# One decoder step on one core: one-pass spreading of the samples' B and C, and a round's eight score products issued as one run

## The chip, the cores and the metric

The kernel runs on one core of one Trainium2 chip. Its engines are TensorE (PE in the rows, with its weight loads as PEld), VectorE (DVE), ScalarE (ACT), GpSimd (POOL) and SyncE (SP), whose queue issues most loads. The metric is the device time of one execution in microseconds; lower is better. Three timed runs of the kernel before gave 1047.99, 1053.06 and 1053.59 us, so the median is 1053.06 us. The profiled execution is a fourth one, of 1040.78 us.

## What is computed

One inference step of a two-layer hybrid decoder, for a prompt of 256 tokens and 8 samples of one token each, which share the weights. The part that matters here is one layer's mixer:

```
h = RMSNorm(x) * (1 + sc1) + sh1
proj = h @ w_in                       # q, six K/V sets, gates, z, x/B/C, dt
o_cmp  = attention over compressed blocks
o_slc  = attention over the selected 64-token blocks
o_win  = attention over the last 512 tokens plus self
o_att  = gates[0] * o_cmp + gates[1] * o_slc + gates[2] * o_win
h_new  = h_old * exp(dt * A) + dt * x (outer) B     # per sample and head
y      = h_new . C + d_skip * x ; y = RMSNorm(y * SiLU(z))
x = x + g1 * (concat(o_att, y) @ w_out)
x = x + g2 * ConvFFN(RMSNorm(x) * (1 + sc2) + sh2)
```

For the samples K and V come from pages of 128 tokens (selected branch, 8 pages a sample) and from a window buffer of 512 tokens a sample. The window buffer is also an output, so each sample's 512 KB are loaded and stored.

## The kernel before

**Stages.** A layer runs in this order: modulation and norm, the input projection, the mixer, the output projection, the FFN. In the profiled execution the first layer's mixer lies from about 165 to 300 us and the second one's from about 670 to 800 us. In the mixer five generators are interleaved by a table of letters (`SEQ`, then `CYCLE`): S is `samples` (attention of the 8 samples), P is `prompt` (attention of the prompt, four heads by two branches), M is the state space chain (`space_prompt`, `space_samples`, `gate`), B the prompt's compressed branch, Z the z projection. A scheduler places each engine's instructions in a fixed order at build time; on the chip each engine takes them in that order and waits where an operand is not there.

**S: three rounds.** A round `i` treats 512 keys of each of the 8 samples: rounds 0 and 1 are four pages each of the selected branch, round 2 is the window. `fetch` loads one sample's keys and values of a round into one of 8 slots (`PAGES`, tile `page`); a slot comes free when the round before has used its values, so the loads of round 2 (`in_wst_dram`, 512 KB each) are issued when `values(1, ...)` is done. With each of these loads `fetch` also issues a store of the same tile (`out_wst_dram`, on POOL's queue), which waits for the load. `scores` makes eight products, one for each sample: `qz` of the sample (128 x 32, as weights) with the sample's 128 x 512 keys, in float32. Their results go to four groups of 32 partitions of one PSUM bank (tile `psat`); samples 2c and 2c+1 add up in group c. Then DVE adds the bank to `sc`, the softmax follows, `transposed` turns the weights around (`psmm<-cst,whi`) and `values` multiplies them with the pages (`psmm<-page,wlo`). A float32 product shows as two MATMUL records in the trace.

**M: the samples' state.** `space_samples` turns the samples' B and C (channels 4 and 5 of `xc`) to 8 rows (`bc`), spreads them on a diagonal (`bds`, tile `mam`, 8 rows x 1024) and makes four products of a matrix of ones with `bds`, one for each of B and C and each half of the heads. These bring every sample's B and C to all 128 partitions, 128 x 512 in PSUM each. DVE multiplies them with `dtx` and with the state, POOL updates the state. `gate` then normalises y (products `psat<-s,cst`, then `row`, `rs`) and multiplies it with the second half of `w_out`.

**`together`** (used for the modulation products already) emits a list of products and holds all but the first to the program's order at high priority, so that they stand in a row on PE.

Of the kernel before, what the change touches and what calls it, by code (L numbers as in the profile page):

```python
# [9 lines left out]
F32 = mybir.dt.float32  # L10
F32R = mybir.dt.float32r
I32 = mybir.dt.int32
AF = mybir.ActivationFunctionType
OP = mybir.AluOpType
# [6 lines left out]
NS = 8  # L21
# [16 lines left out]
def _const_array():  # L38

    parts = []  # L40

    def add(name, a):
        a = np.asarray(a, np.float32)
        b = np.zeros((128, a.shape[1]), np.float32)
        b[:a.shape[0]] = a
        CONST_W[name] = (sum(x.shape[1] for x in parts), b.shape[1])
        parts.append(b)

    i = np.arange(128)
    slopes = 2.0 ** -(np.arange(8) + 1.0)  # L50
    r = i
    c4, rr = r // 32, r % 32
    live = rr < 16
    sp, h = rr // 8, rr % 8
    g = h // 4
    smp = 2 * c4 + sp
    slope = np.where(live, slopes[h], 0.0)
    add("ident", np.eye(128))
    add("one", np.ones((128, 1)))
    tri = (i[:, None] <= i[None, :])  # L60
    add("tri", tri)
    add("tneg", np.where(tri, 0.0, -1e30))
    same = (smp[:, None] == smp[None, :]) & (g[:, None] == g[None, :]) & live[:, None] & live[None, :]
    add("two", np.eye(2).reshape(1, 4).repeat(128, 0))
    add("same", same)
    q, k = i[:, None], i[None, :]
    diag = np.where(q >= k, q - k, 1e30)
    add("dist", np.concatenate([diag, 128.0 + q - k, diag], 1))
    n = np.arange(NCMP)
    add("cbias", -slope[:, None] * (PAST - (16 * n + 31))[None])  # L70
    n = np.arange(15)
    pb = np.zeros((128, 8, 2, 15))
    pm = np.zeros((128, 2, 15))
    for qt in range(2):
        dd = (qt * 128 + i)[:, None] - (16 * n + 31)[None]
        pm[:, qt] = dd >= 0
        for hh in range(8):
            pb[:, hh, qt] = np.where(dd >= 0, -slopes[hh] * dd, -1e30)
    add("pbias", pb.reshape(128, 240))
    add("pmask", pm.reshape(128, 30))  # L80
    add("slope", slope[:, None])
    hm = np.zeros((128, 3, 8))
    hm[i, :, h] = live[:, None]
    add("hmask", hm.reshape(128, 24))
    gcol = np.arange(128) // 64
    gm = (g[:, None] == gcol[None]) & live[:, None]
    add("gmask", gm)
    add("rmask", np.stack([live & (sp == s) for s in range(2)], 1))
    sel = np.zeros((8, 128))
    sel[smp[live], i[live]] = 1.0  # L90
    add("sels", sel)
    ov_n, ov_j = np.arange(NCMP), np.arange(16)
    add("overlap", (16 * ov_n[:, None] < 64 * ov_j[None] + 64) & (16 * ov_n[:, None] + 32 > 64 * ov_j[None]))
    add("sum4", np.tile(np.eye(32), (4, 1)))
    add("iota", np.broadcast_to(np.arange(16.0), (128, 16)))
    return np.concatenate(parts, 1)

# [5 lines left out]
def decode_step(ctx, tc, I, O):  # L103
# [20 lines left out]
    V, S, G, PE = [Pinned(*z) for z in (("DVE", nc.vector), ("ACT", nc.scalar), ("POOL", nc.gpsimd), ("PE", nc.tensor))]  # L124
# [40 lines left out]
    def ph(shape, tag, bufs=1, dt=F32):  # L165
        return sb(shape, tag, bufs, dt, pools[-1])
# [9 lines left out]
    K = {n: cst[:, o:o + w] for n, (o, w) in CONST_W.items()}  # L176
    ident, ones = K["ident"], K["one"].to_broadcast([128, 128])
# [12 lines left out]
    qz = sb([NS, 32], "qz")  # L190
    G.memset(qz, 0.0)

    def split(src, hi, lo):

        S.activation(hi, src, AF.Copy)
        V.tensor_tensor(lo, src, hi.bitcast(F32), op=OP.subtract)
# [16 lines left out]
    def together(calls):  # L213

        for n, (out, w, a, start, stop) in enumerate(calls):
            if n == 0:
                PE.matmul(out, w, a, start=start, stop=stop)
                continue
            with tc.high_priority():
                tc.keep_in_program_order(PE.matmul(out, w, a, start=start, stop=stop))  # L220
# [257 lines left out]
    def layer(l, A, pa, early, done, side, fill):  # L478
        p = PAR[l]
# [20 lines left out]
        order = (0, 2, 4, 6, 1, 3, 5, 7)  # L500
        ring = []
# [133 lines left out]
        def samples():  # L635
# [72 lines left out]

            def scores(i, sc):
                o = sx()  # L710
                for n, s in enumerate(order):
                    c = s // 2
                    PE.matmul(o[32 * c:32 * c + 32, :], qz[:, s, :], ring[NS * i + n][0], start=s % 2 == 0, stop=s % 2 == 1)
                V.tensor_tensor(sc, sc, o, op=OP.add)

            def transposed(sc, pT):
# [266 lines left out]
        def mb():  # L983
            return ps("at", BANKS[0])
# [92 lines left out]
        def space_samples():  # L1077
# [19 lines left out]
            S.activation(dec_s, ov_[:, :, 1, :], AF.Copy)  # L1097
            V.tensor_tensor(dtx, dtx, xc[:, 0:4, 259::4], op=OP.mult)
            o = mb()
            for i in range(2):  # L1100
                PE.transpose(o[:8, i * 128:(i + 1) * 128], xc[:, 4 + i, 259::4], ident)
            bc = small([2, 128], 1, "bc")
            S.activation(bc[:8], o[:8, :256].rearrange("p (b n) -> p b n", b=2), AF.Copy)
            ys = small([4, NS], 1, "ys")
            bds = [ph([1024], "mam", 2) for _ in range(2)]
            for g in range(2):
                V.tensor_tensor(bds[g][:8].rearrange("p (b s n) -> p b s n", b=2, s=NS),
                                bc[:8, :, 64 * g:64 * g + 64].unsqueeze(2).to_broadcast([8, 2, NS, 64]),
                                ident[:8, :8].unsqueeze(1).unsqueeze(3).to_broadcast([8, 2, NS, 64]), op=OP.mult)
            for g in range(2):  # L1110
                yield
                h0 = slot("st", [2, NS, 64])
                load(h0, I["ssm"][l, :, 2 * g:2 * g + 2])
                G.tensor_tensor(h0, h0, dec_s[:, 2 * g:2 * g + 2, :].unsqueeze(3).to_broadcast([128, 2, NS, 64]), op=OP.mult)
                u = slot("st", [2, NS, 64])
                for b in range(2):
                    o = mb()
                    PE.matmul(o, ones[:8, :], bds[g][:8, 512 * b:512 * b + 512], start=True, stop=True)
                    yield
                    ov_ = o.rearrange("p (s n) -> p s n", s=NS)  # L1120
                    for i in range(2):
                        if b == 0:
                            V.tensor_tensor(u[:, i], dtx[:, 2 * g + i, :].unsqueeze(2).to_broadcast([128, NS, 64]), ov_,
                                            op=OP.mult)
                        else:
                            V.tensor_tensor(u[:, i], h0[:, i], ov_, op=OP.mult)
                    if b == 0:
                        G.tensor_tensor(h0, h0, u, op=OP.add)
                        store(O["ssms"][l, :, 2 * g:2 * g + 2], h0)
                V.tensor_reduce(ys[:, 2 * g:2 * g + 2, :], u, axis=AX.X, op=OP.add)  # L1130
# [304 lines left out]
```

## Time and profile before

| | |
|---|---|
| timed runs | 1047.99, 1053.06, 1053.59 us (median 1053.06) |
| profiled execution | 1040.78 us, its span 1039.0 us (1.78 us lie around the span) |
| busy share of the span | PE 91%, PEld 77%, DVE 63%, ACT 47%, POOL 16% |
| mean granted TensorE clock | 0.945 of 2.4 GHz |
| DMA | 220.35 MB, mean 212 GB/s |

An engine's busy time says only how long it had an instruction in work. Of PE it also counts instructions that run at the lower clock (0.50, that is 1.2 GHz). What a change is worth is read in the stretch where it acts: which engine the others wait for there, and what ends that engine's own waits.

### The profile page before, as it was taken

How to read it: one execution, taken by the hardware profiler on the slowest of the kernel's cores; microseconds unless marked ns; L12 is line 12 of the kernel's file. 1: busy time of each engine (PE TensorE's matmuls, PEld its weight loads, DVE VectorE, ACT ScalarE, POOL GpSimd, SP SyncE). 2: the span in 40 equal slices, each digit the busy share in tenths (PEclk: the TensorE clock that was granted, in tenths of full speed). 3: DMA queues.
4: the chain of work that ended last, by engine and by line, in shares of the span. 5: the costliest groups of instructions: out<-in, count | busy, mean ns of one | idle time of the engine just before them, and what ended most of it. 6: DMA issues, size and time to landing. Idle time of an engine off the chain costs nothing.

```text
span 1039.0 us, 21345 instructions
## 1 busy us (share of the span) xinstructions
PE 949.7 (91%) x7864; PEld 803.7 (77%) x7864; DVE 650.7 (63%) x1429; ACT 487.4 (47%) x1042; POOL 167.8 (16%) x337
## 2 busy tenths in 40 slices
PE   4599998988997998999999989998999799999996
PEld 2368997653585998999999868875447599999995
DVE  1386643867677665676754575485665687777553
ACT  1356543533444555555634344454244366666441
POOL 2000100225221101001101112031421221111110
PEclk9699999999997999999999989997599899999998
DMA  9987488246757786756675578725283835666651
GB/s 357 313 278 266 158 265 292 94 129 225 270 171 254 232 301 216 238 194 220 210 251 174 183 279 301 244 83 158 91 354 96 330 124 182 183 183 183 194 163 42
DMA packets 101258, 220.35 MB, mean 212 GB/s; under 512 B 11682, under 2 KB 54562, under 8 KB 101026
## 3 DMA queue, kind: packets, MB, share of 16 engines
q1 hardware_dynamic: 97058, 205.28, 59.8%
q0 software_dynamic: 3520, 13.17, 3.1%
q8 instruction: 62, 1.02, 0.4%
q10 hardware_dynamic: 576, 0.54, 0.2%
q14 instruction: 42, 0.34, 0.1%
HBM read 204.70 MB, written 14.25 MB: 211 GB/s over the span
## 4 chain that ended last, share of the span: by engine, by line
PE 76%; DMA 11%; DVE 7%; ACT 3%; issue 2%; SPq 1%; POOL 0%; DVEq 0%; ACTq 0%; POOLq 0%
PE psmm L117 40%; PE psat L117 22%; PE pso L117 10%; PE psfl L117 4%; DMA st<-in_cw_dram 3%; DMA ada<-in_ada_dram 3%; DVE wlo L117 2%; DMA cpg<-in_ada_dram 2%; DMA st<-in_wup_dram 1%; DMA page<-in_wst_dram 1%; DVE s L117 1%; SPq L117 1%; ACT whi L117 1%; DVE rs L117 1%; ACT psc L117 1%
## 5 line engine op out<-in xcount | busy, mean ns | idle before, releaser
L117 DVE TENSOR_TENSOR wlo<-st,whi 128x1024 fp32r<-128x1024 f32 (+1 forms) x204 | 232.7, 1142 | 152.6 <-ACT whi L117 149.1
L117 ACT ACTIVATE whi<-st 128x1024 fp32r<-128x1024 f32 (+1 forms) x204 | 201.6, 990 | 217.5 <-PE psmm L117 150.2
L117 PE MATMUL psmm<-hhi,whi 128*128 128x264 f32 x800 | 233.7, 293 | 3.3 <-ACT whi L117 1.4
L117 PE MATMUL psmm<-hhi,wlo 128*128 128x264 f32 x800 | 228.5, 286 | 1.1 <-DVE wlo L117 1.1
L117 PE MATMUL psmm<-hlo,whi 128*128 128x264 f32 x800 | 228.2, 286 | 0.0
L117 PEld LDWEIGHTS psmm<-hhi,whi 128*128 128x128 f32 x800 | 151.4, 189 | 17.0 <-ACT whi L117 5.2
L117 PEld LDWEIGHTS psmm<-hhi,wlo 128*128 128x128 f32 x800 | 150.9, 189 | 5.2 <-DVE wlo L117 2.4
L117 PEld LDWEIGHTS psmm<-hlo,whi 128*128 128x128 f32 x800 | 151.5, 190 | 2.4 <-issue 2.0
L117 PE MATMUL psmm<-act,whi 128*128 128x264 f32 x704 | 128.5, 284 | 0.0
L117 PEld LDWEIGHTS psmm<-act,whi 128*128 128x128 f32 x704 | 108.9, 188 | 1.6 <-issue 1.6
L117 PE MATMUL psat<-hhi,whi 128*128 128x264 f32 x352 | 100.8, 286 | 2.2 <-ACT whi L117 2.2
L117 PE MATMUL psat<-hhi,wlo 128*128 128x264 f32 x352 | 100.5, 286 | 1.0 <-DVE wlo L117 1.0
L117 PE MATMUL psat<-hlo,whi 128*128 128x264 f32 x352 | 100.6, 286 | 0.0
L117 PE MATMUL psmm<-act,wlo 128*128 128x264 f32 x352 | 99.9, 284 | 0.0
L117 PE MATMUL pso<-whi,cwh 128*128 128x252 f32 x256 | 74.8, 292 | 8.7 <-ACT whi L117 8.0
L117 PE MATMUL pso<-wlo,cwh 128*128 128x252 f32 x256 | 74.1, 290 | 1.8 <-DVE wlo L117 1.8
L117 PE MATMUL pso<-whi,cwl 128*128 128x252 f32 x256 | 73.6, 287 | 0.0
L117 PEld LDWEIGHTS psat<-hhi,whi 128*128 128x128 f32 x352 | 67.1, 191 | 2.5 <-ACT whi L117 2.5
L117 POOL COPY fout<-xr 128x26 f32<-128x26 f32 x44 | 28.1, 639 | 247.0 <-ACT xr L117 247.0
L117 PEld LDWEIGHTS psat<-hhi,wlo 128*128 128x128 f32 x352 | 66.7, 190 | 1.2 <-DVE wlo L117 1.2
L117 PEld LDWEIGHTS psat<-hlo,whi 128*128 128x128 f32 x352 | 67.2, 191 | 0.0
L117 PEld LDWEIGHTS psmm<-act,wlo 128*128 128x128 f32 x352 | 66.1, 188 | 0.0
(305 smaller groups left out, 1579.5 us busy)
## 6 DMA issues: line engine op xcount, KB each, us to landing
st<-in_wup_dram SPq DMA_DIRECT2D x88, 512.0 KB, 3.9
ada<-in_ada_dram SPq DMA_DIRECT2D x80, 512.0 KB, 5.2
st<-in_wdn_dram SPq DMA_DIRECT2D x44, 512.0 KB, 3.6
st<-in_win_dram SPq DMA_DIRECT2D x40, 512.0 KB, 4.9
page<-in_slcc_dram SPq DMA_DIRECT2D x128, 128.0 KB, 2.7
cpg<-in_ada_dram SPq DMA_DIRECT2D x16, 512.0 KB, 9.4
st<-in_cw_dram SPq DMA_DIRECT2D x16, 512.0 KB, 5.9
cpg<-in_cmpc_dram SPq DMA_DIRECT2D x64, 128.0 KB, 3.7
```

The costliest lines, as they stand in the source:

```text
L117: ins = f(*a, **k)
```

## The change

It has two parts and touches nothing else.

1. **B and C in one pass.** The 16 columns of B and C (8 samples each) are split to a high and a low float32r part and laid side by side (`xs`, 16 columns for B and 16 for C). The transposes then give 16 rows, `eye8` (a new 16 x 8 constant) spreads the high and the low row of each sample, `bds` is of float32r with 16 rows, and the matrix of ones is a float32r copy of 16 rows (`oner`). The four products have 16 rows and float32r operands in place of 8 rows and float32.
2. **A round's scores in one run.** The eight products go through `together`, from the last sample's page to the first's; the products of odd samples now start a partition group and those of even samples end it.

```
+    add("eye8", np.tile(np.eye(8), (2, 1)))
...
             def scores(i, sc):
                 o = sx()
-                for n, s in enumerate(order):
-                    c = s // 2
-                    PE.matmul(o[32 * c:32 * c + 32, :], qz[:, s, :], ring[NS * i + n][0], start=s % 2 == 0, stop=s % 2 == 1)
+                together([(o[32 * (s // 2):32 * (s // 2) + 32, :], qz[:, s, :], ring[NS * i + n][0], s % 2 == 1, s % 2 == 0)
+                          for n, s in reversed(list(enumerate(order)))])
                 V.tensor_tensor(sc, sc, o, op=OP.add)
...
             o = mb()
+
+            xs = ph([2, 16], "xs", 1, F32R)
+            split(xc[:, 4:6, 259::4], xs[:, :, :8], xs[:, :, 8:])
             for i in range(2):
-                PE.transpose(o[:8, i * 128:(i + 1) * 128], xc[:, 4 + i, 259::4], ident)
+                PE.transpose(o[:16, i * 128:(i + 1) * 128], xs[:, i, :].bitcast(F32), ident)
             bc = small([2, 128], 1, "bc")
-            S.activation(bc[:8], o[:8, :256].rearrange("p (b n) -> p b n", b=2), AF.Copy)
+            S.activation(bc[:16], o[:16, :256].rearrange("p (b n) -> p b n", b=2), AF.Copy)
+            oner = ph([128], "oner", 1, F32R)
+            S.activation(oner[:16], ones[:16], AF.Copy)
             ys = small([4, NS], 1, "ys")
-            bds = [ph([1024], "mam", 2) for _ in range(2)]
+            bds = [ph([1024], "mam", 2, F32R) for _ in range(2)]
             for g in range(2):
-                V.tensor_tensor(bds[g][:8].rearrange("p (b s n) -> p b s n", b=2, s=NS),
-                                bc[:8, :, 64 * g:64 * g + 64].unsqueeze(2).to_broadcast([8, 2, NS, 64]),
-                                ident[:8, :8].unsqueeze(1).unsqueeze(3).to_broadcast([8, 2, NS, 64]), op=OP.mult)
+                V.tensor_tensor(bds[g][:16].rearrange("p (b s n) -> p b s n", b=2, s=NS),
+                                bc[:16, :, 64 * g:64 * g + 64].unsqueeze(2).to_broadcast([16, 2, NS, 64]),
+                                K["eye8"][:16].unsqueeze(1).unsqueeze(3).to_broadcast([16, 2, NS, 64]), op=OP.mult)
...
-                    PE.matmul(o, ones[:8, :], bds[g][:8, 512 * b:512 * b + 512], start=True, stop=True)
+                    PE.matmul(o, oner[:16, :], bds[g][:16, 512 * b:512 * b + 512], start=True, stop=True)
```

**Where the instructions stand.** In the fences below, `page_n` are the loaded pages; those of one round bear rising numbers in the order of their loads. The first place is PE in the first layer, at round 1. Before:

```order
L117 MATMUL psat_2734<-mam_2692,cst_61 128x512
L117 MATMUL psat_2886<-page_2753,qz_72 32x512
L117 MATMUL psat_2886<-page_2767,qz_72 32x512
L117 MATMUL psat_2886<-page_2781,qz_72 32x512
L117 MATMUL psat_2886<-page_2795,qz_72 32x512
L117 MATMUL pso_2927<-pT_437_2900,vt_1881 64x256
L117 MATMUL psat_2912<-mam_2692,cst_61 128x512
L117 MATMUL psat_2886<-page_2825,qz_72 32x512
L117 MATMUL pso_2927<-pT_439_2906,vt_1881 64x256
L117 MATMUL pso_2927<-pT_437_2900,vt_1881 64x128
L117 MATMUL pso_2927<-pT_439_2906,vt_1881 64x128
L117 MATMUL psat_2942<-mam_2693,cst_61 128x512
```

Four products stand together and the other four singly, among the products of B and C, up to the last one three rows of the prompt's scores later. The same place now:

```order
L118 MATMUL pso_2932<-pT_441_2911,vt_1881 64x128
L118 MATMUL psat_2891<-page_2872,qz_72 32x512
L118 MATMUL psat_2891<-page_2858,qz_72 32x512
L118 MATMUL psat_2891<-page_2844,qz_72 32x512
L118 MATMUL psat_2891<-page_2830,qz_72 32x512
L118 MATMUL psat_2891<-page_2800,qz_72 32x512
L118 MATMUL psat_2891<-page_2786,qz_72 32x512
L118 MATMUL psat_2891<-page_2772,qz_72 32x512
L118 MATMUL psat_2891<-page_2758,qz_72 32x512
L118 MATMUL psat_2917<-mam_2697,oner_2694 128x512
L118 MATMUL psat_2947<-mam_2698,oner_2694 128x512
```

All eight stand in a row, the page that was loaded last (2872) first. Three of the four products of B and C are behind them; the first of these four and the prompt's values stand ahead.

The second place is PE in the first layer at round 2, the window (`pso<-pT` ends the prompt's values, `psat<-s` and `row` are `gate`'s, `pp`, `kv,q` and `vcp` the prompt's). Before:

```order
L117 MATMUL pso_2927<-pT_465_3055,vt_1881 64x128
L117 MATMUL psat_3035<-page_2967,qz_72 32x512
L117 MATMUL psat_3061<-s_467_3065,cst_61 2x264
L117 MATMUL psat_3061<-s_468_3071,cst_61 2x264
L117 MATMUL psat_3035<-page_2970,qz_72 32x512
L117 MATMUL psat_3061<-s_469_3077,cst_61 2x264
L117 MATMUL psat_3061<-s_470_3083,cst_61 2x264
L117 MATMUL psat_3035<-page_2973,qz_72 32x512
L117 MATMUL psat_3087<-cst_61,row_74 128x2 x3
L117 MATMUL psat_3129<-cst_61,pp_2618 15x128 x4
L117 MATMUL psat_3142<-kv_1450,q_1449 128x128
L117 MATMUL psat_3143<-kv_1450,q_1449 128x128
```

The products of the eight pages are spread over some forty rows of other work, one at a time. Now:

```order
L118 MATMUL pso_2932<-pT_467_3060,vt_1881 64x128
L118 MATMUL psat_3040<-page_3009,qz_72 32x512
L118 MATMUL psat_3040<-page_3006,qz_72 32x512
L118 MATMUL psat_3040<-page_3003,qz_72 32x512
L118 MATMUL psat_3040<-page_3000,qz_72 32x512
L118 MATMUL psat_3040<-page_2981,qz_72 32x512
L118 MATMUL psat_3040<-page_2978,qz_72 32x512
L118 MATMUL psat_3040<-page_2975,qz_72 32x512
L118 MATMUL psat_3040<-page_2972,qz_72 32x512
L118 MATMUL psat_3066<-s_469_3070,cst_61 2x264
L118 MATMUL psat_3066<-s_470_3076,cst_61 2x264
L118 MATMUL psat_3066<-s_471_3082,cst_61 2x264
```

The run of eight stands where the first window product stood before, its first row uses the page that is loaded last (3009), and everything that stood between the eight is now behind them. The second layer has the same order here. The loads of the pages keep their place on SP's queue.

The third place is POOL in the first layer, at the stores of the window pages (`psc<-psc,psm` scales the prompt's weights). Before:

```order
L1129 DMA out_ssms_dram<-st_2938 128x1024
L117 TENSOR_SCALAR psc_3009<-psc_3009,psm_3010 128x128
L117 TENSOR_SCALAR psc_3009<-psc_3009,psm_3010 128x256
L117 TENSOR_SCALAR psc_3009<-psc_3009,psm_3010 128x128
L117 TENSOR_SCALAR psc_3009<-psc_3009,psm_3010 128x256
L511 DMA out_wst_dram<-page_2967 128x1024
L511 DMA out_wst_dram<-page_2970 128x1024
```

Now:

```order
L1134 DMA out_ssms_dram<-st_2943 128x1024
L512 DMA out_wst_dram<-page_2972 128x1024
L512 DMA out_wst_dram<-page_2975 128x1024
L118 TENSOR_SCALAR psc_3014<-psc_3014,psm_3015 128x128
L512 DMA out_wst_dram<-page_2978 128x1024
```

In the first layer the stores begin ahead of the prompt's scaling; in the second they did so before already.

## Rows read from the trace of the kernel before

**Rows 1.** The page's chain that ended last, by engine.

```profile
PE 76%; DMA 11%; DVE 7%; ACT 3%; issue 2%; SPq 1%; POOL 0%; DVEq 0%; ACTq 0%; POOLq 0%
```

**Rows 2.** Stretches: length; busy PE, PEld, DVE, ACT, POOL (count); clock; DMA; GB/s.

```profile
254.00:276.00 22.00, 21.42 (x108) 9.96 (x110) 12.34 (x40) 8.36 (x24) 9.24 (x16) 1.00 1.02 396
752.00:774.00 22.00, 19.73 (x88) 8.04 (x89) 13.52 (x42) 7.97 (x22) 6.45 (x12) 1.00 1.02 408
...
728.00:754.00 26.00, 24.91 (x131) 11.26 (x130) 16.75 (x36) 5.93 (x19) 10.48 (x10) 0.56 0.27 96
...
772.00:798.00 26.00, 23.51 (x209) 16.90 (x209) 15.49 (x52) 12.73 (x39) 3.90 (x9) 0.93 0.28 104
```

**Rows 3.** Timeline of PE, first layer, round 1: start, us, instructions, [idle <-releaser].

```profile
230.59 2.04 PE L117 MATMUL psat<-mam,cst 8*128 8x512 f32 x2 [1.73 <-DVE mam L117]
232.56 1.94 PE L117 MATMUL psat<-page,qz 128*32 128x512 f32 x8
...
235.47 1.12 PE L117 MATMUL psat<-mam,cst 8*128 8x512 f32 x2
236.53 1.04 PE L117 MATMUL psat<-page,qz 128*32 128x512 f32 x2
...
243.19 1.05 PE L117 MATMUL psat<-page,qz 128*32 128x512 f32 x2
```

**Rows 4.** Timeline of PE, second layer, rounds 0 and 1.

```profile
692.07 1.06 PE L117 MATMUL psat<-page,qz 128*32 128x512 f32 x8
...
732.29 3.64 PE L117 MATMUL psat<-page,qz 128*32 128x512 f32 x16
735.86 2.07 PE L117 MATMUL psat<-mam,cst 8*128 8x512 f32 x2
```

**Rows 5.** Timeline of PE, first layer, round 2.

```profile
255.94 1.05 PE L117 MATMUL psat<-page,qz 128*32 128x512 f32 x2
...
272.97 1.04 PE L117 MATMUL psat<-page,qz 128*32 128x512 f32 x2
```

**Rows 6.** Timeline of PE, second layer, round 2.

```profile
754.44 1.02 PE L117 MATMUL psat<-page,qz 128*32 128x512 f32 x2 [0.37 <-DVE wlo L117]
756.27 1.04 PE L117 MATMUL psat<-page,qz 128*32 128x512 f32 x2 [0.82 <-DMA page<-in_wst_dram]
...
771.08 1.04 PE L117 MATMUL psat<-page,qz 128*32 128x512 f32 x2
```

**Rows 7.** Last window loads: duration, first and last start; time to landing; first, second layer.

```profile
L117 SPq DMA_DIRECT2D page<-in_wst_dram x1: 412/412/412, 254.7 to 254.7; - x1
...
DMA to landing us min/median/max: 13.0/13.0/13.0
...
L117 SPq DMA_DIRECT2D page<-in_wst_dram x2: 382/470/557, 753.0 to 753.5; - x2
...
DMA to landing us min/median/max: 14.1/15.1/16.1
```

**Rows 8.** The last load of round 1, first layer, in the same view.

```profile
L117 SPq DMA_DIRECT2D page<-in_slcc_dram x1: 332/332/332, 236.3 to 236.3; - x1
...
DMA to landing us min/median/max: 2.6/2.6/2.6
```

**Rows 9.** Timeline of PE: float32r products in a row.

```profile
276.91 0.29 PE L117 MATMUL psmm<-hhi,whi 128*128 128x264 f32 x1
277.03 0.29 PE L117 MATMUL psmm<-hlo,whi 128*128 128x264 f32 x1
```

**Rows 10.** Timelines of PE and DVE, second layer, before and in round 1.

```profile
720.82 1.03 PE L117 MATMUL psat<-cst,pp 128*15 128x128 f32 x4 [3.68 <-DVE pp L117]
...
741.45 0.69 DVE L117 TENSOR_TENSOR st<-dtx,psat 128x512 f32<-128x512 f32 x1 [3.35 <-PE psat L117]
```

**Rows 11.** Stretches around the clock's falls, columns as in rows 2.

```profile
230.00:235.00 5.00, 4.41 (x12) 0.98 (x12) 5.00 (x10) 0.00 (x0) 0.00 (x0) 0.50 0.73 212
235.00:240.00 5.00, 5.00 (x16) 1.33 (x14) 4.42 (x5) 1.86 (x8) 3.10 (x2) 0.95 0.86 251
```

## The prediction, made before the changed kernel was run

> **What bounds the kernel now.** I read the chain of waits first: three quarters of what ended last is PE [rows 1]. So I went to the two stretches that the change touches and asked, with the busy times by stretch, whether PE is short there too. At the window round it is: in the first layer PE works 21.42 of 22 us, in the second 19.73 of 22, at full clock, while the DMA engines are full (1.02) at some 400 GB/s [rows 2]. So the window pages arrive slowly, and PE doesn't wait for them, because other work stands between the eight products and each takes its turn when its page is there. At round 1 of the second layer PE works 24.91 of 26 us at a mean clock of 0.56 [rows 2], so there it is short of time because it is slow.
>
> **Part 1, one pass.** A product of B and C takes 1.06 us at full clock (start to start, 235.47 to 236.53) and about 2 us at the lower one [rows 3, 4]. No row shows a float32r product of 512 columns; products of 264 columns follow each other every 0.12 us [rows 9], so 512 columns should take 0.23 us at full clock and 0.47 at half; bounds are these and the old price. Four products per layer: in the second layer 4 x (2.0 - 0.47) = 6.1 us of PE. There PE is the one that the others wait for: DVE sat idle 3.35 us for such a product, and the samples' softmax stood behind it in DVE's queue [rows 10]. I take 5 us earlier there, between 3 and 6.5. In the first layer the saving is about 4 us of PE, but see the next part. The additions (a split of 128 x 32 elements on ACT and DVE, a copy of 16 rows, 16 in place of 8 rows in the transposes and in `bds`) lie beside the input projection or change only the count of partitions; I cost them at nothing. Their cover is PE's product work; without it they are three small operations, at most 1 us a layer.
>
> **Part 2, rounds 0 and 1.** One page product alone is 1.04 us [rows 3]; four in a row, which go to four different partition groups, take 1.06 us together, and eight 3.64 us at the lower clock [rows 4]. So a run of eight costs 2.1 us at full clock and 3.6 at half. Beside this row stands a rule of the Trainium skill (TensorE: Matmul & The Clock Gate, Part 3, on packing small matmuls): three column tiles of width 32 with 512 columns gave 2.38 times, not 3. By that, four in a row would take 1.3 us and a run of eight 2.6, which adds 0.5 us a run at full clock; the row of this kernel shows four for the price of one, and I go by the row.
>
> Round 0 has all its pages in time; it saves about 1 us of PE in each layer, half of which I count: -1 us in all (0 to -2). In round 1 of the second layer the eight stood in a row already, nothing changes. In round 1 of the first layer the last page's load was issued at 236.3 us and landed 2.6 us later, at 238.9 [rows 8]; SP's order is as before. The run now stands ahead of three of the products of B and C, so PE waits for 238.9, runs eight at the lower clock and ends at 242.5, where the last single product before ended at 243.19 + 1.05 = 244.2 [rows 3]. That is 1.7 us sooner for the samples, but the products of B and C come later, and DVE, which was busy 9.4 of 10 us here [rows 11], gets its work later. I take 1 us sooner (0 to 3).
>
> **Part 2, round 2, where the sum is made.** Now the run of eight stands where the first window product stood, and its first product needs the last page. PE takes its products in order, so everything that stood between the eight waits too: `gate`'s products and its chain of small DVE operations, the prompt's scores, transposes and values; behind these wait the second half of the output projection, and on POOL and ACT the prompt's softmax. PE came to this point at 255.94 us in the first layer and at 754.07 in the second (754.44 less 0.37 idle), and was through with the last page product at 274.0 and 772.1: 18.1 and 18.0 us [rows 5, 6]. The last page landed at 254.7 + 13.0 = 267.7 and 753.5 + 16.1 = 769.6 [rows 7].
>
> Of these 18 us the page products are up to 8 x 1.04 = 8.3, PE's idle time 0.6 and 2.3 (from the 22 us of [rows 2]); some page products ran beside `gate`'s narrow ones, so the displaced work is 9.2 to 11 us in the first layer (I take 10) and 7.4 to 9 in the second (8.2). Now:
> First layer: wait 11.8 us, if the page lands as before, to 14.9, if it takes 16.1 us from its issue as in the second, where the stores began early; the order on POOL now starts the stores as early in both. I take 13.3. The run of eight after such a wait goes at the lower clock, 3.6 (2.1 to 3.6): before, an idle time of 3.68 us [rows 10] preceded the fall whose mean of 0.56 is in [rows 2]. Displaced work 10; the clock was back within about 5 us in the first layer (0.50, then 0.95) [rows 11], so half of 5 us is lost, 2.5 (0 to 5). Sum 13.3 + 3.6 + 10 + 2.5 = 29.4 against 18.1: 11.3 later, less the 1 us of round 1: +10.3 (+2 to +16).
> Second layer: 15.5 (to 16.3) + 3.6 + 8.2 + 2.5 = 29.8 against 18.0: 11.8 later, less 5: +6.8 (+0.5 to +13).
> What of this is given back later: after the round PE still had 2.5 us of idle time in the second layer (26 less 23.51) [rows 2], which work on DVE, ACT and DMA done during the wait can fill; -2.5 in all. Beyond that PE is busy to the end of the mixer, and the FFN's loads follow the slots that PE frees, so a late mixer is a late kernel.
>
> Sum: +10.3 + 6.8 - 1 - 2.5 = +13.6 us. Against the profiled execution's own time 1040.78 that is 1054.4. The median of the timed runs is 12.3 us above that execution; I add the difference to the median: 1053.06 + 13.6 = 1066.7, say 1067. The ends of the terms give -2 to +29.
>
> **Rivals.** About 0.5%, 5.3 us, is what a measurement of this kernel can tell from no change.
> 1. The loads outrun the stores, and the kernel gets faster. Loads and stores of a round are 4.19 MB each; at the 408 GB/s of [rows 2] both take 20.6 us and the loads alone 10.3. Were the stores held back, the last page could land about 6 us sooner in each layer; PE would be idle for so short a time that less clock is lost, 4 us a layer with the run at 2.1. That gives 13.6 - 12 - 8 = -6, 1047 us. It decides once the two waits fall under some 7.6 us each, where the sum is zero. For it: the first layer's page landed sooner when the stores were late. Against it: POOL's order now has two stores ahead of its other work in both layers. Chance 0.08.
> 2. The stall is there, but the terms lie at their low ends (clock back at once, 5 us or more gained in round 1): 0 to +5, about 1056. For it: PE's work becomes some 10 us less in each layer, so what is idle is partly paid by what is saved. Chance 0.14.
> 3. The clock stays low through all the displaced work. Before round 2 of the second layer it stayed low through 20 us of just such narrow products, with PE busy 24.91 of 26 us [rows 2]. Then the displaced 18.2 us count twice: 18.2 - 5 more, +27, 1080 us. Against it: at the window round before, the same work ran at 1.00 [rows 2], though with no long wait ahead of it. Beside it stands a rule of the Trainium skill (the same page, in its section on what matters for kernels) that speaks against this change: idle gaps between bursts of products are to be avoided, since the clock falls in them. That falls in the wait is in my forecast; the rule doesn't say how soon work like this brings the clock back. Chance 0.14.
> That the change doesn't do what it says is no rival: the order on PE shows the eight in a row.
>
> **How the numbers follow.** The forecast, +5.3 to +23, has 0.64. Slower is the forecast and rival 3, 0.78; same is rival 2, 0.14; faster is rival 1, 0.08. The range 1051 to 1082 is the terms' own ends on the median; it leaves out most of rival 1, a part of rival 3 and the forecast's tail, under 2 in 10.
>
> **What would show it.** In the trace after: one idle time of PE of 11 to 16 us in each layer ahead of `psat<-page,qz`, released by the DMA of a window page; the lower clock in that stretch; another wait of about 6 us in the first layer's round 1, on a page of the selected branch; products of B and C at 0.25 to 0.5 us; eight page products in 2 to 3.6 us. The forecast is wrong if the last window page lands within 8 us of PE's coming there, or if PE's idle time after the round shrinks by much more than 2.5 us, which would say that the stall was covered by waits that I have not seen.

## The result, and the profile of the changed kernel

The changed kernel is slower: 1055.97 us in the median of 20 runs, against 1045.58 us in the median of 20 runs of the kernel before. The ratio is 1.0124, with a 95% interval from 1.0098 to 1.0149, so about 13 us; the forecast was +13.6. The two profiled executions, 1056.25 and 1040.78 us, stand 15.5 us apart. This ratio, like those below, leaves out runs that took over 1.5% longer than the shortest of the same kernel (five of the kernel before, none of the changed one); the medians of all 20 are 10.4 us apart. Each ratio below is taken with runs of the kernel before that were made on the same chip in the same hour. Their medians were 1041.63, 1048.93 and 1046.72 us for the three groups of experiments, so ratios are to be compared and not microseconds.

The chain that ended last has shifted from PE to DMA by one per cent each [rows 1]:

```profile
PE 75%; DMA 12%; DVE 6%; ACT 2%; SPq 2%; issue 2%; POOL 0%; ACTq 0%; DVEq 0%; POOLq 0%
```

The same chain in order of time (start, length, what it was) has one link in each layer that is the last window page on its way from its issue, 33.4 us in all. In the kernel before it has one alone, in the second layer. First that one, then the two of the changed kernel:

```profile
752.46 10.99 DMA page<-in_wst_dram
```

```profile
254.90 16.50 DMA page<-in_wst_dram
...
762.86 16.93 DMA page<-in_wst_dram
```

The timeline of PE (start, length, instructions, [idle before <-releaser]), to be laid beside [rows 3 to 6], first layer, then second layer:

```profile
238.81 3.87 PE L118 MATMUL psat<-page,qz 128*32 128x512 f32 x16 [3.58 <-DMA page<-in_slcc_dram]
...
253.69 1.57 PE L118 MATMUL pso<-pT,vt 128*64 128x256 f32 x8
271.54 3.64 PE L118 MATMUL psat<-page,qz 128*32 128x512 f32 x16 [16.27 <-DMA page<-in_wst_dram]
274.98 2.17 PE L118 MATMUL psat<-s,cst 128*2 128x264 f32 x8
...
290.64 0.39 PE L118 MATMUL psmm<-hhi,whi 128*128 128x264 f32 x1
...
329.07 1.04 PE L118 MATMUL psat<-row,cst 128*1 128x264 f32 x2 [4.70 <-POOL row L118]
...
706.77 1.92 PE L118 MATMUL psat<-page,qz 128*32 128x512 f32 x16
...
736.15 1.03 PE L118 MATMUL psat<-cst,pp 128*15 128x128 f32 x4 [3.81 <-DVE pp L118]
...
750.47 0.95 PE L118 MATMUL psat<-mam,oner 16*128 16x512 f32 x3
...
754.29 0.76 PE L118 MATMUL psat<-kv,q 64*128 64x128 f32 x2 [2.02 <-DVE sm L118]
...
762.13 1.57 PE L118 MATMUL pso<-pT,vt 128*64 128x256 f32 x8
779.92 3.64 PE L118 MATMUL psat<-page,qz 128*32 128x512 f32 x16 [16.21 <-DMA page<-in_wst_dram]
783.36 2.27 PE L118 MATMUL psat<-s,cst 128*2 128x264 f32 x8
...
799.12 0.39 PE L118 MATMUL psmm<-hhi,whi 128*128 128x264 f32 x1
```

Before the window's run PE stands still for 16.3 us in each layer. In the kernel before, the same stretch had PE busy for 21.42 of 22 us in the first layer and 19.73 of 22 in the second [rows 2]. By stretches (length; busy PE, PEld, DVE, ACT, POOL; clock; DMA; GB/s), the wait, the run and the work behind it:

```profile
255.30:271.50 16.20, 0.00 (x0) 0.00 (x0) 3.80 (x13) 2.64 (x10) 4.08 (x8) 0.59 1.02 414
271.50:275.00 3.50, 3.46 (x17) 0.84 (x18) 0.00 (x0) 0.00 (x0) 1.80 (x4) 0.50 1.04 416
275.00:287.00 12.00, 10.92 (x71) 6.69 (x67) 9.15 (x36) 5.66 (x18) 0.57 (x2) 0.98 0.21 83
...
763.80:779.90 16.10, 0.00 (x0) 0.01 (x1) 3.76 (x13) 2.58 (x10) 4.05 (x8) 0.60 1.02 416
779.90:784.00 4.10, 4.08 (x18) 1.06 (x19) 0.32 (x1) 0.00 (x0) 1.80 (x4) 0.50 1.04 415
784.00:796.00 12.00, 10.93 (x70) 6.68 (x67) 9.35 (x37) 6.18 (x20) 1.09 (x3) 1.00 0.15 58
```

During the wait PE does nothing, DVE, ACT and POOL are busy for about a quarter of it or less, and the DMA engines move 414 and 416 GB/s; the run goes at the lower clock (0.50), the work behind it at 0.98 and 1.00.

To follow the difference through the kernel I laid the start of the same product in both timelines beside each other. The marks are the first products of the second half of `w_out`, behind each window round, and the first row of the first layer's FFN norm; in the kernel before they stand here:

```profile
276.43 0.39 PE L117 MATMUL psmm<-hhi,whi 128*128 128x264 f32 x1
...
315.86 1.04 PE L117 MATMUL psat<-row,cst 128*1 128x264 f32 x2 [4.35 <-POOL row L117]
...
777.37 0.37 PE L117 MATMUL psmm<-hhi,whi 128*128 128x264 f32 x1
```

With the rows above this gives the account of the pair. The changed kernel was 1.7 us ahead where the first mixer began (167.02 against 168.75), by nothing that the change touches. It is one execution of each: over the profiled executions of all kernels here, that start lies anywhere from 167.0 to 171.1 us.

| stretch | later by (us) | worked out as |
|---|---|---|
| first mixer up to the window round | +1.0 | PE there at 253.69 + 1.57 = 255.26 against 255.94 [rows 5], that is -0.7, from -1.7 |
| first window round | +14.9 | 290.64 - 276.43 = +14.2, from -0.7 |
| from there to the FFN | -1.0 | 329.07 - 315.86 = +13.2 |
| FFN, second layer up to round 1 | +2.1 | 736.15 - 720.82 [rows 10] = +15.3 |
| second layer, round 1 | -5.7 | 762.13 + 1.57 = 763.70 against 754.07, +9.6 |
| second window round | +12.1 | 799.12 - 777.37 = +21.75 |
| from there to the end | -6.2 | spans 1054.5 - 1039.0 = +15.5 |

### The profile page after: what moved, and what is told of

Read it like the earlier page. It is cut to its first block, busy times and chain, and to the rows that moved or that the text cites. A ratio compares the mean times of both kernels' runs of the same rounds, so it can differ in the third digit from the quotient of the medians.

```text
span 1054.5 us, 21302 instructions
## 1 busy us (share of the span) xinstructions
PE 929.7 (88%) x7856; PEld 805.4 (76%) x7856; DVE 651.2 (62%) x1431; ACT 488.9 (46%) x1046; POOL 166.6 (16%) x337
## 4 chain that ended last, share of the span: by engine, by line
PE 75%; DMA 12%; DVE 6%; ACT 2%; SPq 2%; issue 2%; POOL 0%; ACTq 0%; DVEq 0%; POOLq 0%
PE psmm L118 40%; PE psat L118 21%; PE pso L118 10%; PE psfl L118 4%; DMA ada<-in_ada_dram 3%; DMA page<-in_wst_dram 3%; DMA st<-in_cw_dram 3%; SPq L118 2%; DVE wlo L118 2%; DMA cst<-in_consts_dram 1%; DVE rs L118 1%; ACT whi L118 1%; DMA st<-in_wup_dram 1%; DVE s L118 1%; DMA x<-in_xT_dram 0%
## 5 line engine op out<-in xcount | busy, mean ns | idle before, releaser
L118 PEld LDWEIGHTS psmm<-hhi,whi 128*128 128x128 f32 x800 | 151.3, 189 | 14.9 <-issue 5.1
```

What stands on the lines that cost most here:

```text
L118: ins = f(*a, **k)
```

## Experiments

The theory on record says that the loss is PE's wait at the window round: the run stands where the first window product stood, its first product needs the page that lands last, and all that PE could do meanwhile stands behind it. The rivals: part 1 itself costs; round 1's run costs; the price is the lower clock and not the wait; the stores make the page late.

### The two parts apart

`e1_onepass_alone` keeps part 1 and puts the old loop back:

```
-                together([(...) for n, s in reversed(list(enumerate(order)))])
+                for n, s in enumerate(order):
+                    c = s // 2
+                    PE.matmul(o[32 * c:32 * c + 32, :], qz[:, s, :], ring[NS * i + n][0], start=s % 2 == 0, stop=s % 2 == 1)
```

> Part 1 alone: B and C in one pass, the scores issued singly as in the kernel before. Theory (all of the loss is made by the window's run of eight, part 1 only gains): 5 to 8 us faster than before, a ratio of 0.992 to 0.995; PE's products of B and C 0.22 to 0.5 us each; no PE idle time over 3 us at the window round. Rival A (the split, the 16 rows or a shift of order cost something, and part 1 is itself a part of the loss): no gain or slower, 1.000 or more.

Measured: 1.0001, from 0.9973 to 1.0029. Neither the gain of 5 to 8 us nor a clear loss: at most 3 us either way. The trace shows where a part of the saving went. In the first layer a product then waits for its page, and in the second for the samples' own softmax (the rows at 724.59 and 752.99 are marks around the second layer's round 1):

```profile
242.77 1.89 PE L118 MATMUL psat<-page,qz 128*32 128x512 f32 x2 [2.66 <-DMA page<-in_slcc_dram]
...
724.59 1.03 PE L118 MATMUL psat<-cst,pp 128*15 128x128 f32 x4 [3.52 <-DVE pp L118]
...
744.15 1.07 PE L118 MATMUL psmm<-cst,whi 128*128 128x128 f32 x4 [1.82 <-ACT whi L118]
...
746.37 1.65 PE L118 MATMUL psat<-kv,q 64*128 64x128 f32 x4 [1.16 <-DVE st L118]
...
752.99 1.57 PE L118 MATMUL pso<-pT,vt 128*64 128x256 f32 x8
```

Between the two marks it is 3.3 us shorter than before (28.40 us from start to start, 31.67 before). But from the first FFN's norm row to the second mixer's first product this execution took 360.5 us against 356.8, which part 1 doesn't touch. In the other profiled executions that stretch takes 357.3 to 361.6 us, the kernel before having the shortest, so one pair of profiles doesn't settle 3 us.

`e2_runs_alone` is the changed kernel with part 1 undone (8 rows of float32 in place of 16 of float32r).

> Part 2 alone: the three rounds' scores as runs of eight, last page first, B and C in float32 as before. Theory: the loss of the whole change plus the gain of part 1, 15 to 22 us slower than before, 1.015 to 1.021, with one PE idle time of 14 to 17 us in each layer at the window round. Rival A (part 1 carries the loss): within 4 us of before.

Measured: 1.0171, from 1.0132 to 1.0209, with idle times of PE of 13.48 and 16.11 us at the two window rounds. So part 2 carries the loss, as expected. The second layer's round 1, with B and C in float32:

```profile
737.96 1.03 PE L117 MATMUL psat<-cst,pp 128*15 128x128 f32 x4 [3.81 <-DVE pp L117]
...
752.48 3.05 PE L117 MATMUL psat<-mam,cst 8*128 8x512 f32 x6
...
763.81 1.57 PE L117 MATMUL pso<-pT,vt 128*64 128x256 f32 x8
```

From mark to mark that is 25.85 us, as short as in the changed kernel (762.13 - 736.15 = 25.98) without part 1. The clock is the same too (the round in the changed kernel, then here, columns as in the stretches above):

```profile
736.20:763.70 27.50, 22.37 (x162) 12.66 (x162) 19.50 (x41) 8.48 (x26) 11.48 (x11) 0.69 0.50 147
```

```profile
738.00:765.40 27.40, 24.21 (x166) 12.84 (x166) 19.52 (x41) 8.33 (x26) 11.81 (x11) 0.69 0.48 149
```

### Which round

`e3_window_single` has runs in rounds 0 and 1 alone (`if i < 2: together(...)`, else the old loop), `e4_round0_alone` in round 0 alone (`if i == 0`), `e14_window_run_alone` in the window round alone (`if i == 2`).

> The changed kernel, but the window round's eight products singly as before; rounds 0 and 1 as runs. Theory (the wait at the window round is the whole loss): 5 to 10 us faster than before, 0.990 to 0.995, and 18 to 24 us faster than the changed kernel; the PE idle times of 16 us are gone. Rival B (the loss is in the wait on the selected page in round 1 and in the clock after it): still 3 us or more slower than before.

Measured: 1.0113, from 1.0065 to 1.0161: the window was single and the kernel was still slower. By the first theory that couldn't be. It was run again beside others:

> The kernel with runs in rounds 0 and 1 and the window single, once more, beside the kernels it is to be compared with. Theory (its first timing was right: its window products wait for pages that share the DMA with stores that now begin earlier, and the clock falls in those waits): 1.005 to 1.014. Rival (the first timing was a matter of that chip and hour; its profile, only 4.6 us over that of before, was the better guide): 0.997 to 1.004.

Measured: 1.0059, from 1.0022 to 1.0096. So there is a loss, 0.6 or 1.1% by the two timings; their intervals together reach from 0.2 to 1.6%.

> The changed kernel, but only round 0's scores as a run; rounds 1 and 2 singly as before. One-pass B and C alone gave 1.000, and with runs in rounds 0 and 1 the kernel was at 1.011 although the window was single. Theory (round 1's run makes that loss: it waits for the last page of its round, and the pages of the window and their stores then meet PE in another rhythm): round 0 is free, 0.997 to 1.003. Rival (round 0's run, which changes the order of everything behind it, already costs): 1.006 or more.

Measured: 0.9977, from 0.9939 to 1.0015. Round 0's run is free. In the second layer the traces show what it saves: from the mixer's first product to the mark `psat<-cst,pp` it took 48.1 us in the three kernels with round 0 single (48.12 before) and 47.0 in all others but one (47.01 in the changed kernel; 47.5 in `e12_little_later_and_held`).

> One-pass B and C, rounds 0 and 1 singly as before, only the window's eight as a run at its early place. Theory (the window's run carries the loss by its wait, whatever rounds 0 and 1 do): one idle time of 12 to 13 us in the first layer, where the stores stand behind POOL's scaling as before, 16 in the second; 1.006 to 1.014. Rival (round 1's run carries the loss, as the kernel with the window single at 1.011 says): 0.997 to 1.003.

Measured: 1.0097, from 1.0061 to 1.0133. The window's run alone does carry a loss by its wait. The waits are somewhat shorter than expected (POOL's scaling stands ahead of the stores in the first layer here, as before):

```profile
271.81 3.64 PE L118 MATMUL psat<-page,qz 128*32 128x512 f32 x16 [11.48 <-DMA page<-in_wst_dram]
...
785.83 3.53 PE L118 MATMUL psat<-page,qz 128*32 128x512 f32 x16 [14.33 <-DMA page<-in_wst_dram]
```

So two things cost time here, each without the other: the window as an early run, and round 1 as a run with a single window behind it. Whether they add up can't be told from ratios this wide; together they are at 1.0124.

### The wait at the window round

`e10_run_later` is the changed kernel with the run moved two turns of S later:

```
-WAITS = (0, 0, 0, 1, 1)
+WAITS = (0, 0, 2, 1, 1)
```

`gate`'s first products and most of the prompt's scores then stand ahead of the run on PE.

> The changed kernel, but the window's run of eight stands two turns of the samples later, behind the gate's first products and the prompt's scores. The stores are as in the changed kernel. Theory (the wait's length is the price): the same last page lands at the same time, PE does 8 to 10 us of the displaced work meanwhile and idles 5 to 8 us, 1.000 to 1.006. Rival (a shorter wait brings nothing, since the clock falls all the same): 1.009 or more.

Measured: 0.9978, from 0.9942 to 1.0013. One number moved, and 1.0124 became 0.998, with the stores as in the changed kernel. The waits were even shorter than I expected:

```profile
274.71 3.22 PE L118 MATMUL psat<-page,qz 128*32 128x512 f32 x16 [0.60 <-DMA page<-in_wst_dram]
...
779.09 3.62 PE L118 MATMUL psat<-page,qz 128*32 128x512 f32 x16
```

`e6_stores_held` leaves the run where it is and holds the stores:

```
-                store(O["wst"][l, s], t)
+                late.append((O["wst"][l, s], t))
...
             scores(2, sc)
+            t = late[-1][1]
+            tc.keep_in_program_order(G.tensor_copy(t[:, 0:1], t[:, 0:1]))
+            for z in late:
+                tc.keep_in_program_order(store(*z))
```

PE's order is that of the changed kernel, row for row.

> The changed kernel, but the eight stores of the window pages wait until the window's run of eight is through (a copy of one column of the last page on POOL, the stores behind it). Theory (the wait's length is the price, and the stores make up about 6 us of it): the last page lands 9 to 11 us after its issue in place of 16.5, PE's idle time ahead of the run is 8 to 11 us in place of 16, and the kernel is at 1.000 to 1.006. Rival (the price is the lower clock around the wait, whatever its length, as two waits of 6 and 2 us seemed to say): 1.009 or more.

Measured: 0.9983, from 0.9947 to 1.0019. The window loads' time from issue to landing (shortest, median, longest, first layer), first in the changed kernel, then with the stores held; and in a third fence PE's timeline with the stores held (the first view counts one store as well; of the loads alone the median is 9.5):

```profile
DMA to landing us min/median/max: 3.8/8.5/16.5
```

```profile
DMA to landing us min/median/max: 3.6/8.2/11.2
```

```profile
267.20 3.64 PE L119 MATMUL psat<-page,qz 128*32 128x512 f32 x16 [10.67 <-DMA page<-in_wst_dram]
...
770.61 3.64 PE L119 MATMUL psat<-page,qz 128*32 128x512 f32 x16 [9.95 <-DMA page<-in_wst_dram]
```

The stores made up 5.6 and 6.3 us of the waits, the 6 us of my first rival. Waits of some 10 us cost nothing on balance here. What is saved on PE is of that size: up to 8.3 us of single page products become a run of 3.44 in each layer, and the second layer's round 1 was 5.7 us shorter in the changed kernel.

`e5_window_in_fours` splits the window's run (pages 4 to 1, then 8 to 5):

```
+                    for half in ((3, 2, 1, 0), (7, 6, 5, 4)):
+                        together([(..., order[n] % 2 == 0, order[n] % 2 == 1) for n in half])
```

> The changed kernel, but the window round as two runs of four, pages 4 to 1 at the old place of the run, pages 8 to 5 some rows later, behind the gate's first products. Theory: the first run waits for the fourth page, which lands about half way, 6 to 9 us of PE idle time per layer, and the second run waits again for a part of the rest, 2 to 6 us; in all 0 to 8 us slower than before, 1.000 to 1.008. Rival C (the price is that of any wait, through the lower clock behind it, and not that of the length of the wait): as slow as the changed kernel, 1.010 or more.

Measured: 1.0141, from 1.0103 to 1.0180. The waits are about those expected, 5.96 and 1.95 us in the first layer, and the kernel is as slow as with 16. The two runs on the timeline of PE, and then the stretches from the first run to the end of the second and behind it (first layer), and behind the second run (second layer):

```profile
262.25 1.94 PE L119 MATMUL psat<-page,qz 128*32 128x512 f32 x8 [5.96 <-DMA page<-in_wst_dram]
...
271.68 1.93 PE L119 MATMUL psat<-page,qz 128*32 128x512 f32 x8 [1.95 <-DMA page<-in_wst_dram]
```

```profile
262.20:273.50 11.30, 8.79 (x38) 2.80 (x38) 2.26 (x12) 0.59 (x1) 3.41 (x7) 0.65 1.03 418
273.50:291.00 17.50, 16.83 (x66) 9.60 (x64) 10.65 (x31) 7.15 (x23) 2.58 (x6) 0.50 0.26 101
...
779.00:797.00 18.00, 17.33 (x67) 9.84 (x67) 10.65 (x31) 7.84 (x26) 2.39 (x5) 0.53 0.28 113
```

In the changed kernel the work behind the run went at 0.98 and 1.00; here it goes at 0.50 and 0.53 for some 17 us with PE busy all the time. Half the wait, but the displaced work at half the clock: that is my third rival, in another kernel. So the wait's length alone doesn't set the loss. How this clock is decided after a wait is not told by these rows.

### What is late next

Two kernels combine the cures. `e11_later_and_held` has `WAITS[2]` = 2 and the stores held, `e12_little_later_and_held` has `WAITS[2]` = 1 and the stores held.

> Both: the window's run two turns later and the stores behind it. Theory: the last page is there when PE comes, an idle time of 0 to 2 us, the run of eight takes 2.0 to 2.2 us at full clock, and what is left is the saving of the runs and of one pass: 0.988 to 0.996, the fastest of all. Rival (round 1's run alone costs 1 per cent, as with the window single): 1.003 or more.

Measured: 1.0084, from 1.0051 to 1.0117. No wait for a page is left, as expected, and still it is slow. POOL's copy stands behind more scaling there and the stores leave from 285 us on; they fill the DMA engines when the next weights are wanted. ACT's `whi` waits 5.68 us for a load of `w_out` there, in `e10_run_later` 0.6 at most (a stretch, and two rows of PE's timeline):

```profile
292.00:302.00 10.00, 6.23 (x42) 5.41 (x43) 3.22 (x10) 2.99 (x6) 0.00 (x0) 0.86 0.92 350
```

```profile
299.95 0.59 PE L119 MATMUL psmm<-hhi,whi 128*128 128x264 f32 x1 [3.68 <-ACT whi L119]
...
311.44 0.33 PE L119 MATMUL psat<-cst,ovw 128*128 128x128 f32 x1 [2.09 <-DVE ovw L119]
```

The last row is the samples' tail, which now stands at the mixer's end with nothing beside it; `e10_run_later` shows the same 2.09 us.

> The changed kernel with the window's run one turn later, behind the gate's first products and their chain but ahead of the prompt's scores, and the stores held. Theory: the wait of 10 us that held stores alone leave shrinks by the 6 to 7 us of the gate's chain, to 2 to 5 us, and the samples' tail does not stand bare at the mixer's end as with two turns; 0.988 to 0.995, faster than both kernels. Rival (the tail or the held stores cost as much as the wait gives): 0.998 or more.

Measured: 1.0030, from 0.9997 to 1.0063, so my expectation failed. The page is there, but three other waits have taken its place in each layer:

```profile
256.95 3.58 PE L119 MATMUL psat<-s,cst 128*2 128x264 f32 x8 [2.94 <-ACT s L119]
...
264.33 3.42 PE L119 MATMUL psmm<-cst,rs 128*128 128x128 f32 x12 [2.47 <-DVE rs L119]
...
281.50 1.91 PE L119 MATMUL pso<-pT,vt 128*64 128x256 f32 x8 [2.39 <-ACT pT L119]
```

`gate`'s chain (`s`, `rs`) and the prompt's softmax (`pT`) have latencies of their own, and in the kernel before single page products stood in them: there PE was idle 1.0 us for `pT`, 0.5 us for `row` and not at all for `s` or `rs` in the first layer's round. Together the three are 7.8 us, in place of the 10.67 us for the page. The last row's products also went slower, 1.91 us where the same eight took 1.25 in the changed kernel (289.46 us); how much of the missing gain is the clock was not taken apart.

`e7_single_and_held` is the kernel with the window single and runs in rounds 0 and 1, with the stores held.

> The same kernel with the stores of the window pages held behind the window's scores. Theory (the stores that share the DMA cause its loss): the single products wait under 1 us in all for pages in the first layer and under 2 in the second, and the kernel is 8 us or more faster than without the hold, 0.992 to 0.999. Rival (its loss lies elsewhere, in round 1 or in the gate's products that stand behind later pages): within 3 us of the kernel without the hold.

Measured: 0.9960, from 0.9923 to 0.9997, the lowest ratio of all and just faster than the kernel before, though 0.9977, 0.9978 and 0.9983 lie within its interval; without the hold it was 1.0059 in the same hour. PE's order is the same in both, row for row. From 250 to 270 us in the first layer: two fences without the hold, a stretch and PE's waits for window pages in it (us in all, times, longest), then two with the hold:

```profile
250.00:270.00 20.00, 16.08 (x55) 5.38 (x55) 10.29 (x36) 4.87 (x16) 5.67 (x10) 0.80 1.02 393
```

```profile
PE psat L118 <- DMA page<-in_wst_dram: 3.8, 3, 1.4
```

```profile
250.00:270.00 20.00, 17.04 (x94) 6.74 (x86) 12.59 (x40) 5.33 (x16) 3.73 (x8) 1.00 0.76 290
```

```profile
PE psat L119 <- DMA page<-in_wst_dram: 2.3, 4, 1.4
```

So the hold gives back what the kernel with a run in round 1 loses, and with PE's order the same, what costs is the stores' share of the DMA engines. The waits themselves differ by 1.5 us only in this stretch; the clock, 0.80 against 1.00, differs with them. From the last `pso<-pT` ahead of the window to the first product of the second half of `w_out` the hold saves 5.3 us in the first layer (33.91 to 28.61) and 3.5 in the second (32.19 to 28.68).

Why the loss comes with round 1's run is less clear. In the first layer that run moves the stores ahead of POOL's scaling; in the second their order on POOL is that of before. In both it changes PE's order: `gate`'s `row` products stand behind the fifth page there, in the kernel before behind the third and the fourth. And the kernel before with its stores held was not run, so it is not shown that the hold would gain nothing in the old order too.

## Why the prediction was right, and where it was off

**The sign, the size and the place** were right: +13.6 forecast, about +13 by the ratio, +10.4 by the medians, +15.5 in the profiled pair, and each layer shows the one idle time before `psat<-page,qz`, released by a window page. That the sum came so near is in part luck: in the profiled pair the first mixer up to the mark cost 15.9 us in place of 10.3, and 7.2 were given back in place of 2.5. That the wait carries the loss is shown from three sides: the window's run alone brings it (1.0097), the same run later loses it (0.998), pages that land 6 us sooner lose it (0.998).

**The waits.** Forecast 13.3 and 15.5 us, measured 16.27 and 16.21. The second lies at its upper end, the first above it (14.9). The step that was too low is the first layer's middle value between late and early stores, and the price of early ones: with late stores the wait was 11.48 us, as I had it (11.8), with early ones 16.27.

**The run and the work behind it.** The run of eight took 274.98 - 271.54 = 3.44 us at the lower clock, forecast 3.6. At full clock eight took 1.92 us (706.77), forecast 2.1. By the Trainium skill's factor for three column tiles (TensorE: Matmul & The Clock Gate, Part 3 on packing small matmuls) the estimate was 2.6; the row of this kernel decides. For the displaced work I had 10 and 8.2 us, and 2.5 more each for a clock that stays low a while. From the run's end to the mark it took 290.64 - 274.98 = 15.66 and 799.12 - 783.36 = 15.76 us, of which 276.43 - 274.0 = 2.4 and 777.37 - 772.1 = 5.3 came behind the last page product before. That leaves 13.2 and 10.5, against 12.5 and 10.7. The sizes hold, but not their reason: the clock was back at once (0.98, 1.00), and the rest is the displaced work itself, with its own small waits. Sum of the window rounds: +14.9 and +12.1, forecast +11.3 and +11.8.

**Round 1.** In the second layer round 1 got 5.7 us shorter, forecast 5, but the number agrees by luck: I put it down to part 1, and without part 1 (`e2_runs_alone`) it is as short. What both have in common against the kernel before is the clock: in this round its mean was 0.56 before [rows 2] and 0.69 in both. Part 1 did what I said on PE, three products in 0.95 us where `e2_runs_alone` took 3.05, but the 2 us come back as a wait of 2.02 us for the samples' softmax (754.29). In the first layer I had 1 us sooner and got 1.0 later, with round 0 in it. PE waited 3.58 us for the selected page, where I had about 6, and the run began at 238.81, as forecast; round 1 itself was 2.5 us shorter, and the time was lost ahead of it. There PE went at 0.50 from 219 us on, where the kernel before had 1.00 up to 227.9, and it came 3.4 us later, counted from the mixer's start, to the first product of B and C. That the change causes this is not shown: `e1_onepass_alone` and `e14_window_run_alone` have one order on PE up to the window round and took 62.8 and 66.7 us for this stretch. Round 0, forecast at -1 us, is free within what a ratio can tell (0.9977, up to 1.0015), and saves 1.1 us in the second layer. The larger miss is that I costed round 1's run on PE alone. It moves POOL's stores, which I had seen and put down to the last page's landing only, and the window's single products; with the window single it costs 0.6 to 1.1%.

**What is given back later.** Forecast 2.5 us, measured 1.0 behind the first round and 6.2 behind the second. Against it stand 2.1 us in the FFN and the next layer's first part, which I had not foreseen: 1.1 less by round 0's run and 3.2 more in the stretch to the second mixer's first product. For the 3.2 no cause is shown; the kernel before had the shortest such stretch of all profiled executions.

**The base.** 1067 was 11 us over the measured median. Most of it is the last step: I added 12.3 us because the median of three runs stood so far above the profiled execution. Of 20 runs the median is 1045.58, so 7.5 us of that were chance; the other 3.2 are +13.6 against +10.4. The profiled execution's own sum, 1054.4, is within 2 us of the profiled execution after, 1056.25.

**The rivals.** The first had its size right (6 us of each wait) and its mechanism in a kernel that holds the stores, where the loss vanishes but no gain is shown. It was to decide under waits of 7.6 us; the held stores came out even at 10.67 and 9.95. The second, low ends, didn't happen. The third didn't happen in the changed kernel, and did when the run was split in two.

## What to carry to other kernels

A run of products needs its last operand first if it is written from the last page to the first; before joining single products to a run, ask what stood between them, since it hid the transfer and they hid its waits. Put the run where its last operand has landed, not where its first one used to be wanted. And look at what the new order does on the queues of the idle engines: stores under way beside loads that PE needs can cost as much as a long wait (1.0059 with them, 0.996 with the stores held).

## What the runs showed of the hardware

**Stores issued behind the loads delayed them.** With stores under way the last window page landed 16.5 us after its issue, with the stores held 11.2; in the first case the DMA engines moved 414 GB/s. The Trainium skill (DMA: Bandwidth & Descriptors, on queues, rings and completion order) says that an engine goes round the queues that have work, packet by packet. The trace agrees in so far as the stores, the first of them issued with the last load at 254.9 us, landed 6.1 to 7.4 us after their issue, the first four of them ahead of the last page; turns by the packet no run here shows.

**Much the same work ran at either clock behind a wait.** After one idle time of 16.27 us and a run of eight at 0.50 the work behind went at 0.98 (0.91 to 1.00 in both layers of the three other kernels with the run at that place). After idle times of 5.96 and 1.95 us, with PE busy 8.79 of 11.30 us from the first run on, it went at 0.50 for 17.5 us. I had counted on the lower clock behind the long wait.

**Times of one kernel spread with their mean clock.** 17 runs of the kernel before in one hour lie between 1035.01 us, at a mean granted clock of 0.952, and 1058.39 us, at 0.925. The median of three runs was 7.5 us off that of twenty, over half of the effect that was looked for here.
